# A fourth column tile in the opening rounds of an encoder layer's kernel, and y's second row tile loaded one slot sooner

## The chip, the cores and the metric

The kernel runs on one core of one Trainium2 chip. The metric is the time of one execution on the device in microseconds (us), the median of three runs. Five engines work beside each other, each in its own order, and wait for one another by semaphores: TensorE (PE; PEld is its weight load), VectorE (DVE), ScalarE (ACT), GpSimd (POOL) and SyncE (SP), which issues all DMAs here, one after the other.

## The reference

One layer of an encoder over 2048 tokens (a grid of 32 rows by 64 columns) of width 1024, in float32. In short:

```python
mod = silu(c) @ ada_w + ada_b                # shift, scale, gate
h = layernorm(x) * (1 + scale) + shift       # (2048, 1024)
proj = h @ w_in                              # (2048, 9216)
q_h, i_h, zf_fw, zf_bw, g_h, q_n, k_n, v_n, g_n = split(proj)
y_hg = hgrn2(q_h, i_h, zf_fw, zf_bw) * silu(g_h)       # 8 heads of 128, both directions
y_na = neighbourhood_attention(q_n, k_n, v_n, rpb) * silu(g_n)   # 16 heads of 64
y = concat(y_hg, y_na) @ w_out               # (2048, 2048) @ (2048, 1024)
x = layernorm(2**0.25 * x + gate * y) * ln_g + ln_b
```

## The kernel before

**Numbers.** A product in float32 is made of three matmuls: each operand is split into a high part (`hi`, a copy rounded to the format float32r, on ACT) and a low part (`lo`, the rest, a subtraction on DVE), and high x high, high x low and low x high are added up in PSUM. `proj_mm` (L274) does these three for one group k of 128 of the 1024 input columns and 512 tokens (128x512 each); eight such groups make one column tile of 128 projected columns. `vproj` (L280) does the same for the values, with 256 columns at a time.

**Stages.** The 2048 tokens are worked on in two halves of 1024, and each half in two groups g of 512. `startup` (L1181) makes h of the first half's groups 0 and 1 and projects the first attention pair (a pair is two attention heads; columns of keys, queries and gate, `NCOL0`) and its values. `first_half` (L1291) runs the attention of the first half for pairs 0 to 7 and, between its steps, projects the columns of the next pair (`first_stream`, L857). The linear recurrence of all heads follows, then the attention of the second half (phase `n1`, L1540) and the output part (phase `wo`, L1580): y, read back from DRAM, times w_out.

**The opening rounds.** The loop at L1261 goes over (g, k), 16 rounds. A round does, in the order of the code: its `jobs` (L1235: weight splits, sums of the modulation on DVE, statistics of x; in (0, 7) the rest of the statistics of group 1, its rates and the scaling of its rows); the four transposes of the next round's x (`turn_`, L232), its h on ACT (`high`, L237 and L239) and the low part on DVE (`low`, L1218); the nine matmuls of its own block, three column tiles i; in the last round of a group the evacuation of the three sums on ACT (`evac`, L772); and a step of `vproj`. In this stage the orders of PE, SP, ACT and DVE are those of the code (`manual_schedule`, L1387). So in (0, 7) PE comes to the transposes of round (1, 0), which need rows of group 1 that are scaled (L225), before it comes to the block of (0, 7).

**The stream of weights.** `Chunks` (L803) loads raw weight chunks of 128x512 through four buffers (`wraw`), splits them into four pairs of buffers (`whi`, `wlo`), and loads the next when one is split; `free` and `tick` say when.

**The weave.** In the later stages only PE's order is the code's; the other engines and SP's queue are ordered by a planner that works with estimates of times and with priorities. `weave` (L1359) lays pieces of a stream of projections between the steps of attention by a cost of 0.68 for each `proj_mm` (`KUS`) and a total; in `first_half` (L1338) the total of a stream is 48 such pieces (`NLEN`), and 10 of them go ahead of pair 0's first step. One attention tile is made of `scores` (L1023: matmuls, then minimum, powers and shares on DVE and ACT), `turned` (L1078: transposes, then copies of the turned probabilities on DVE, L1089, and ACT, L1091) and `sums` (L1095: matmuls with the values, L1107).

**Before the output part.** While pair 6 of the second half runs (u = 6, L1564), its `extra` jobs by slot load and split the first rows of w_out (`wo_load`, `wo_split`), and load the first row tiles of y (`y_early`, L1457, through the same four `wraw` buffers). A row tile is 128 tokens; the early part of a tile is two loads of 128x512 (q = 0, 1). `y_split` (L1462) makes the high parts on ACT (L1467) and the low parts on DVE (L1468). With u = 7, tile 1 is split and the stream between the attention steps is the first half of the output product for row tiles 0 to 3 (`out_stream`, L1486). Its weights on SP are the loads of L1430, the bias tables those of L730 to L738.

Of the kernel before, what the change touches and what calls it, by code (L numbers as in the profile page):

```python
# [11 lines left out]
F32R = mybir.dt.float32r  # L12
# [26 lines left out]
def body(ctx: ExitStack, tc: tile.TileContext, t):  # L39
# [240 lines left out]
    def vproj(src, dst, half, feed=None, fine=False):  # L280
        his, los = feed.take(4) if feed else load_split(lambda i: src[:, i * 512:(i + 1) * 512], 4)
        for t2 in range(2):
            pzs = [ps("pj"), ps("pj")]
            for k in range(KT):
                wh, wl = (w[k // 2][:, (k % 2) * 256:(k % 2 + 1) * 256] for w in (his, los))
                for tp in range(2):
                    for i in range(2):
                        g, o = divmod(((t2 * 2 + tp) * 2 + i) * P, GRP)
                        hh, hl = (hts[g, k, s][:, o:o + P] for s in range(2))
                        for n, (a, b) in enumerate(((hh, wh), (hh, wl), (hl, wh))):  # L290
                            pe.matmul(pzs[tp][:, i * 256:(i + 1) * 256], a, b, start=(k == 0 and n == 0 and i == 0), stop=(k == KT - 1 and n == 2), skip_group_check=True)  # L291
                if k % 2:
                    if k == KT - 1:
                        for tp, pz in enumerate(pzs):
                            v = tl("vo")
                            with tc.high_priority(offset=PRI):
                                (pinned if half else lambda x: x)(act.activation(v, pz, AF.Copy))
                                r0 = half * HALF + (t2 * 2 + tp) * 256
                                dma(dst[r0:r0 + 256].rearrange("(i p) c -> p i c", p=P), v.rearrange("p (i c) -> p i c", c=256))
                    if feed and t2:  # L300
                        feed.free(1)
                if fine or k % 2:
                    yield None
# [553 lines left out]
    def first_stream(st, feed):  # L857
# [6 lines left out]
        for n, c in NCOL0:  # L864
            his, los = feed.take(2)
            for g in range(2):
                pz = ps("pj")
                for k in range(KT):
                    proj_mm(pz, his, los, g, k)
                    if k == KT - 1:  # L870
                        st.raws[n][g] = evac(pz)
                        todo = [(n, g)]
                    if g == 1 and k % 4 == 3:
                        feed.free()
                    feed.tick()
                    if k == 1 and todo:
                        st.piece(*todo.pop())
                    yield KUS
# [302 lines left out]
    def startup():  # L1181
# [47 lines left out]
        for i in range(4):  # L1229
# [9 lines left out]
            (0, 3): [(mod_sum, 4), (w_split, 1, 1), (w_split, 2, 1)],  # L1239
            (0, 4): [(feed.split, 0), (mod_sum, 5)],  # L1240
            (0, 5): [(mod_sum, 6), (stat, 1, 0), (feed.split, 0)],
            (0, 6): [(mod_sum, 7), (stat, 1, 1)],
            (0, 7): [(stat, 1, 2), (stat, 1, 3), (rates, 1), (scale, 1, 0, 2)],
            (1, 2): [(scale, 1, 1, 4)],
        }
# [8 lines left out]
        values = vproj(t["w_v"][0], nv_d[0], 0, feed, True)  # L1254
        rows = {n: [None, None] for n, _ in NCOL0}
        order = [(g, k) for g in range(2) for k in range(KT)]
        turn_(0, 0)
        high(0, 0)
        w_split(0, 0)
        low(0, 0)  # L1260
        for n, (g, k) in enumerate(order):  # L1261
            for f, *a in jobs.get((g, k), []):
                f(*a)
            nxt = order[n + 1] if n + 1 < len(order) else None
            if nxt:
                turn_(*nxt)
            if nxt:
                high(*nxt)
                low(*nxt)
            if (g, k) == (0, 7):  # L1270
                feed.load(8)
                rp = bias_rows()
# [3 lines left out]
            if (g, k) == (1, 0):  # L1276
# [1 line left out]
                bias_tables(rp)  # L1278
                bias_pair(0)
                dma(c_d.rearrange("(p k) -> p k", k=KT), mod["c8"])  # L1280
            for i in (2, 0, 1) if g else (0, 1, 2):
                proj_mm(acc[i, g], *ws[i], g, k)
            if k == KT - 1:
                for i in range(3):
                    rows[NCOL0[i][0]][g] = evac(acc[i, g])
            next(values, None)
            if g:
                feed.tick()
        return rows, feed

    def first_half(raws, feed):  # L1291

        st = Prep(0, 0, raws)
        for n, g in (("k", 0), ("k", 1), ("q", 0), ("g", 0), ("q", 1), ("g", 1)):
# [39 lines left out]
        for w in range(8):  # L1334
            extra = {i: slots[4 * w + i] for i in range(4)}
            if w < 7:
                nxt = Prep(w + 1, 0, {n: [None, None] for n, _ in NCOL})
                dense, total, steps = first_stream(nxt, feed), NLEN + (0 if w % 2 == 0 else VLEN), 8  # L1338
            else:
                nxt, dense, total, steps = None, hgrn_dense(0, 0, feed=feed), HTOT, 10  # L1340
            r = weave(natten_woven(st, nxt, pipe, extra, w == 7), dense, total, steps, ahead=0 if w else AHEAD * KUS)[1]
# [43 lines left out]
    h_alloc()  # L1385
    with psum_phase("n0", NPS), tc.manual_schedule(engines={mybir.EngineType.PE}):
        with phase("st", SB_, SMS), tc.manual_schedule(engines={getattr(mybir.EngineType, e) for e in ("PE", "SP", "Activation", "DVE")}):  # L1387
            raws, feed = startup()
        with phase("n0", NB0, SM0):
            natten_init(4, 0)  # L1390
            st = first_half(raws, feed)

    def reload(g):
        for k in range(KT):
# [145 lines left out]
    with psum_phase("n1", NPS), phase("n1", NB1, SM1), tc.manual_schedule(engines={mybir.EngineType.PE}):  # L1540
# [15 lines left out]
        for u in range(8):  # L1556
            nxt, extra = None, None
            if u < 7:
# [4 lines left out]
                nxt = Prep(u + 1, 1, raws)  # L1563
                if u == 6:  # L1564
                    extra = {4: [(wo_load, 0, 0, 1)], 5: [(wo_load, 0, 2, 3, 4, 5)], 7: [(wo_split, 0, 0, 1)], 8: [(wo_split, 0, 2, 3), (wo_load, 0, 6, 7)],
                             9: [(y_early, 0), (wo_split, 0, 4, 5)], 10: [(y_split, 0), (wo_load, 1, 0, 1, 4, 5), (y_early, 1)]}
            else:
                y_split(1)
                dense, total = out_stream(list(range(NE))), NE * 16 * KUS
# [80 lines left out]
```

## Time and profile before

| | |
|---|---|
| median of 3 runs | 2619.01 us (2618.38 to 2622.39) |
| the profiled execution | 2618.81 us, span 2617.0 us |
| mean granted clock of TensorE | 0.993 |
| busy in the span | PE 2561.1 us, DVE 1736.9, ACT 1435.0, POOL 108.5 |
| DMA | 295.87 MB, mean 113 GB/s |

All times in the profile are from one execution, in us from the start of its span, those of single instructions also in ns. A timeline row has start, duration, engine, line, operation, what it writes and reads, its shape, the number of like instructions merged, and in brackets the idle time of the engine before it with what ended it. A row of waits has who waited for whom, total, number and longest. A row of windows has the stretch, its length, for each engine the busy time and the number of instructions, then the granted clock of TensorE as a share of full speed, the busy share of the DMA engines and the GB/s that they moved. A row of the chain has start, duration and what the path to the end went through. Matmuls are pipelined, and the durations shown overlap.

### The profile page before, as it was taken

How to read it: one execution, taken by the hardware profiler on the slowest of the kernel's cores; microseconds unless marked ns; L12 is line 12 of the kernel's file. 1: busy time of each engine (PE TensorE's matmuls, PEld its weight loads, DVE VectorE, ACT ScalarE, POOL GpSimd, SP SyncE). 2: the span in 40 equal slices, each digit the busy share in tenths (PEclk: the TensorE clock that was granted, in tenths of full speed). 3: DMA queues.
4: the chain of work that ended last, by engine and by line, in shares of the span. 5: the costliest groups of instructions: out<-in, count | busy, mean ns of one | idle time of the engine just before them, and what ended most of it. 6: DMA issues, size and time to landing. Idle time of an engine off the chain costs nothing.

```text
span 2617.0 us, 45804 instructions
## 1 busy us (share of the span) xinstructions
PE 2561.1 (98%) x17140; PEld 2146.7 (82%) x17140; DVE 1736.9 (66%) x4354; ACT 1435.0 (55%) x2857; POOL 108.5 (4%) x143
## 2 busy tenths in 40 slices
PE   6999999999999999999999999999999999899998
PEld 5888888878888888888888888898888887788887
DVE  7444545477777778877787788555777778558443
ACT  4533435376666566666766666455677777431110
POOL 0000000000000000000000000000000000042221
PEclk8999999999999999999999999999999999999999
DMA  7476455212211126212112222345455556443331
GB/s 273 141 211 143 128 169 152 97 55 72 65 65 58 65 69 213 90 49 81 62 60 71 74 80 73 113 125 153 129 137 144 137 139 171 126 153 129 97 97 57
DMA packets 225631, 295.87 MB, mean 113 GB/s; under 512 B 28807, under 2 KB 117511, under 8 KB 224263
## 3 DMA queue, kind: packets, MB, share of 16 engines
q1 hardware_dynamic: 225407, 292.93, 37.0%
q8 instruction: 135, 2.21, 0.4%
q14 instruction: 89, 0.73, 0.1%
HBM read 217.65 MB, written 66.99 MB: 109 GB/s over the span
## 4 chain that ended last, share of the span: by engine, by line
PE 90%; DVE 4%; DMA 3%; ACT 2%; issue 1%; SPq 0%; DVEq 0%; ACTq 0%
PE pj L278 51%; PE pj L291 5%; PE ps L1475 4%; PE ps L1477 4%; PE ps L1476 4%; PE ps L1107 3%; PE ps L1085 3%; PE ps L480 2%; PE ps L472 2%; PE ps L1036 1%; PE ps L547 1%; DMA bias<-tint 1%; PE ps L571 1%; PE ps L1043 1%; PE ps L573 1%; PE ps L519 1%
## 5 line engine op out<-in xcount | busy, mean ns | idle before, releaser
L278 PE MATMUL pj<-h,wh 128*128 128x512 f32 x4000 | 1274.4, 400 | 4.1 <-ACT wh L823 1.9
L278 PEld LDWEIGHTS pj<-h,wh 128*128 128x128 f32 x4000 | 725.7, 188 | 156.5 <-issue 13.8
L278 PE MATMUL pj<-h,wl 128*128 128x512 f32 x2000 | 784.6, 392 | 0.0
L278 PEld LDWEIGHTS pj<-h,wl 128*128 128x128 f32 x2000 | 376.0, 188 | 83.4 <-DVE wl L799 0.4
L1057 ACT ACTIVATE pbuf<-pbuf,mx 128x480 f32<-128x480 f32 (+5 forms) x256 | 152.4, 596 | 114.1 <-DVE mx L1052 113.2
L1052 DVE CUSTOM_DVE_ANT_1 pbuf<-ps,bias 128x480 f32<-128x480 f32 (+5 forms) x256 | 129.1, 540 | 101.0 <-PE ps L1041 43.2
L291 PE MATMUL pj<-wh,h 128*128 128x256 f32 x1024 | 195.7, 286 | 0.3 <-ACT e L772 0.3
L291 PEld LDWEIGHTS pj<-wh,h 128*128 128x128 f32 x1024 | 163.0, 191 | 4.0 <-issue 1.3
L269 DVE TENSOR_TENSOR wl<-wr,wh 128x512 fp32r<-128x512 f32 x192 | 131.3, 684 | 47.7 <-ACT wh L268 46.9
L268 ACT ACTIVATE wh<-wr 128x512 fp32r<-128x512 f32 x192 | 120.2, 626 | 73.7 <-PE pj L278 66.1
L291 PE MATMUL pj<-wl,h 128*128 128x256 f32 x512 | 144.7, 283 | 0.0
L1091 ACT ACTIVATE pt<-ps 120x384 f32<-120x384 f32 (+3 forms) x128 | 65.3, 510 | 119.1 <-PE ps L1085 118.7
L1089 DVE COPY pt<-ps 120x384 f32<-120x384 f32 (+3 forms) x128 | 74.9, 585 | 66.7 <-PE ps L1085 65.7
L1085 PE MATMUL ps<-ident,pbuf 128*128 128x128 f32 (+2 forms) x832 | 113.0, 273 | 4.5 <-DVE pbuf L1062 3.3
L1085 PEld LDWEIGHTS ps<-ident,pbuf 128*128 128x128 f32 (+2 forms) x832 | 96.5, 136 | 22.8 <-issue 2.3
L466 DVE TENSOR_TENSOR de<-e,de 128x512 f32<-128x512 f32 x64 | 44.2, 690 | 95.4 <-ACT de L465 95.4
L1451 ACT ACTIVATE yh<-yr 128x512 fp32r<-128x512 f32 x52 | 32.7, 628 | 132.9 <-PE ps L1476 115.7
L772 ACT ACTIVATE e<-pj 128x512 f32<-128x512 f32 x98 | 58.4, 596 | 82.9 <-PE pj L278 74.3
L1062 DVE TENSOR_SCALAR pbuf<-pbuf,mx 128x480 f32<-128x480 f32 (+5 forms) x256 | 101.0, 412 | 3.8
L1524 DVE TENSOR_TENSOR vt<-ps,gt 128x512 f32<-128x512 f32 x24 | 16.5, 692 | 130.5 <-PE ps L1477 130.5
L291 PEld LDWEIGHTS pj<-wl,h 128*128 128x128 f32 x512 | 97.9, 191 | 1.4 <-issue 0.5
L447 DVE TENSOR_TENSOR_SCAN c<-c,g 128x128 f32<-128x128 f32 x256 | 88.4, 404 | 10.7 <-ACT c L437 10.7
(277 smaller groups left out, 4684.4 us busy)
## 6 DMA issues: line engine op xcount, KB each, us to landing
wr<-in_w_in SPq DMA_DIRECT2D x276, 256.0 KB
yr<-yq SPq DMA_DIRECT2D x64, 256.0 KB
bias<-tint SPq DMA_DIRECT2D x24, 480.0 KB
x<-in_x SPq DMA_DIRECT2D x32, 256.0 KB
ada<-in_ada_m SPq DMA_DIRECT2D x8, 1024.0 KB
wr<-in_w_v SPq DMA_DIRECT2D x32, 256.0 KB
nv<-vt SPq DMA_DIRECT2D x32, 256.0 KB
hs<-s SPq DMA_DIRECT2D x32, 256.0 KB
```

Of the source, the lines that this page charges most:

```text
L268: act.activation(hi, raw, AF.Copy)
L269: dve.tensor_tensor(lo, raw, hi, op=ALU.subtract)
L278: pe.matmul(pz, a, b, start=(k == 0 and n == 0), stop=(k == KT - 1 and n == 2))
L291: pe.matmul(pzs[tp][:, i * 256:(i + 1) * 256], a, b, start=(k == 0 and n == 0 and i == 0), stop=(k == KT - 1 and n == 2), skip_group_check ...
L447: dve.tensor_tensor_scan(c[:, sl], c[:, sl], L[:, sl], 0.0, op0=ALU.add, op1=ALU.subtract)
L1052: return dve.tensor_tensor_reduce(s[:, 0:nk].rearrange("p (r c) -> p r c", c=kw), sc[:, 0:nk].rearrange("p (r c) -> p r c", c=kw), bt[:, 0 ...
L1057: act.activation(s[:, 0:nk], s[:, 0:nk], AF.Exp, scale=-1.0, bias=mx[:, 0:1], accum_out=mx[:, 1:2])
L1062: dve.tensor_scalar(s[:, 0:nk], s[:, 0:nk], mx[:, 2:3], 1.0, op0=ALU.mult, op1=ALU.mult)
L1085: pe.transpose(ptp[0:cw, c * P:(c + 1) * P], s[:, c * cw:(c + 1) * cw], ident)
L1475: pe.matmul(pz, yh[:, kk], wh, start=first, stop=False)
L1476: pe.matmul(pz, yh[:, kk], wl, start=False, stop=False)
L1477: pe.matmul(pz, yl[:, kk], wh, start=False, stop=last)
```

## The change

In `startup`, two more loads fetch the key columns of pair 1 (behind the last load of modulation weights). Their split into high parts is a new first job of round (0, 6) (`fourth_split`, ACT); the low parts follow in (0, 7) (`fourth_low`, DVE). Round (0, 7) has a new order: 14 matmuls of the fourth tile with high weights (k = 0 to 6); its own block, with each evacuation right behind its column tile; the jobs (statistics, rates, scaling of group 1); the small loads; the step of `vproj`; the two high matmuls of k = 7; the fourth tile's low parts on DVE; the transposes and h of round (1, 0); eight matmuls with low weights; the evacuation of the fourth tile; the evacuation of the values. To that end `vproj` yields once more before its last evacuation, and the loop drains it at its end. In group 1 too the evacuations stand right behind each column tile. The sum, `first`, is handed to `first_half`: `first_stream` of pair 1 leaves out the 24 matmuls of its first column tile and group 0, and the total for `weave` is 8 pieces less with w = 0.

In phase `n1`, `y_early` for row tile 1 moves from the end of slot 10 into slot 9, with row tile 0, and so ahead of four loads of w_out (`wo_load`, 1, 0, 1, 4, 5).

```diff
@@ -290,6 +290,8 @@
                         for n, (a, b) in enumerate(((hh, wh), (hh, wl), (hl, wh))):
                             pe.matmul(pzs[tp][:, i * 256:(i + 1) * 256], a, b, start=(k == 0 and n == 0 and i == 0), stop=(k == KT - 1 and n == 2), skip_group_check=True)
                 if k % 2:
+                    if fine and k == KT - 1:
+                        yield None
                     if k == KT - 1:
                         for tp, pz in enumerate(pzs):
                             v = tl("vo")
@@ -864,6 +866,9 @@
         for n, c in NCOL0:
             his, los = feed.take(2)
             for g in range(2):
+                if st.raws[n][g]:
+                    todo = [(n, g)]
+                    continue
                 pz = ps("pj")
                 for k in range(KT):
                     proj_mm(pz, his, los, g, k)
@@ -1239,7 +1244,7 @@
             (0, 3): [(mod_sum, 4), (w_split, 1, 1), (w_split, 2, 1)],
             (0, 4): [(feed.split, 0), (mod_sum, 5)],
             (0, 5): [(mod_sum, 6), (stat, 1, 0), (feed.split, 0)],
-            (0, 6): [(mod_sum, 7), (stat, 1, 1)],
+            (0, 6): [(lambda: fourth_split(),), (mod_sum, 7), (stat, 1, 1)],
             (0, 7): [(stat, 1, 2), (stat, 1, 3), (rates, 1), (scale, 1, 0, 2)],
             (1, 2): [(scale, 1, 1, 4)],
         }
@@ -1254,19 +1259,55 @@
         values = vproj(t["w_v"][0], nv_d[0], 0, feed, True)
         rows = {n: [None, None] for n, _ in NCOL0}
         order = [(g, k) for g in range(2) for k in range(KT)]
+        fourth, fraw = ([], []), [tl("raw"), tl("raw")]
+        for a in range(2):
+            dma(fraw[a], t["w_in"][NCOL0[0][1] // P + 1][:, a * 512:(a + 1) * 512])
+
+        def fourth_split():
+            w = tl("ada", F32R, [P, 2 * D])
+            for a in range(2):
+                hi, lo = (w[:, o:o + 512] for o in (a * 512, D + a * 512))
+                act.activation(hi, fraw[a], AF.Copy)
+                fourth[0].append(hi)
+                fourth[1].append(lo)
+
+        def fourth_low():
+            for a in range(2):
+                dve.tensor_tensor(fourth[1][a], fraw[a], fourth[0][a], op=ALU.subtract)
+
+        def fourth_mm(pz, k, low):
+            wh, wl = (w[k // 4][:, (k % 4) * P:(k % 4 + 1) * P] for w in fourth)
+            for n, (a, b) in enumerate(((wl, hts[0, k, 0]),) if low else ((wh, hts[0, k, 0]), (wh, hts[0, k, 1]))):
+                pe.matmul(pz, a, b, start=(k + n + low == 0), stop=(low == 1 and k == KT - 1))
+
+        def block(g, k):
+            for i in (2, 0, 1) if g else (0, 1, 2):
+                proj_mm(acc[i, g], *ws[i], g, k)
+                if k == KT - 1:
+                    rows[NCOL0[i][0]][g] = evac(acc[i, g])
+
         turn_(0, 0)
         high(0, 0)
         w_split(0, 0)
         low(0, 0)
         for n, (g, k) in enumerate(order):
+            if (g, k) == (0, 7):
+                pz = ps("po")
+                for kx in range(KT - 1):
+                    fourth_mm(pz, kx, 0)
+                block(g, k)
             for f, *a in jobs.get((g, k), []):
                 f(*a)
             nxt = order[n + 1] if n + 1 < len(order) else None
-            if nxt:
-                turn_(*nxt)
-            if nxt:
-                high(*nxt)
-                low(*nxt)
+
+            def ahead():
+                if nxt:
+                    turn_(*nxt)
+                    high(*nxt)
+                    low(*nxt)
+
+            if (g, k) != (0, 7):
+                ahead()
             if (g, k) == (0, 7):
                 feed.load(8)
                 rp = bias_rows()
@@ -1278,17 +1319,26 @@
                 bias_tables(rp)
                 bias_pair(0)
                 dma(c_d.rearrange("(p k) -> p k", k=KT), mod["c8"])
-            for i in (2, 0, 1) if g else (0, 1, 2):
-                proj_mm(acc[i, g], *ws[i], g, k)
-            if k == KT - 1:
-                for i in range(3):
-                    rows[NCOL0[i][0]][g] = evac(acc[i, g])
-            next(values, None)
+            if (g, k) != (0, 7):
+                block(g, k)
+            if (g, k) == (0, 7):
+                next(values)
+                fourth_mm(pz, k, 0)
+                fourth_low()
+                ahead()
+                for kx in range(KT):
+                    fourth_mm(pz, kx, 1)
+                first = evac(pz)
+                next(values)
+            else:
+                next(values, None)
             if g:
                 feed.tick()
-        return rows, feed
-
-    def first_half(raws, feed):
+        for _ in values:
+            pass
+        return rows, feed, first
+
+    def first_half(raws, feed, first):
 
         st = Prep(0, 0, raws)
         for n, g in (("k", 0), ("k", 1), ("q", 0), ("g", 0), ("q", 1), ("g", 1)):
@@ -1335,7 +1385,9 @@
             extra = {i: slots[4 * w + i] for i in range(4)}
             if w < 7:
                 nxt = Prep(w + 1, 0, {n: [None, None] for n, _ in NCOL})
-                dense, total, steps = first_stream(nxt, feed), NLEN + (0 if w % 2 == 0 else VLEN), 8
+                if w == 0:
+                    nxt.raws["k"][0] = first
+                dense, total, steps = first_stream(nxt, feed), NLEN + (0 if w % 2 == 0 else VLEN) - (0 if w else KT * KUS), 8
             else:
                 nxt, dense, total, steps = None, hgrn_dense(0, 0, feed=feed), HTOT, 10
             r = weave(natten_woven(st, nxt, pipe, extra, w == 7), dense, total, steps, ahead=0 if w else AHEAD * KUS)[1]
@@ -1385,10 +1437,10 @@
     h_alloc()
     with psum_phase("n0", NPS), tc.manual_schedule(engines={mybir.EngineType.PE}):
         with phase("st", SB_, SMS), tc.manual_schedule(engines={getattr(mybir.EngineType, e) for e in ("PE", "SP", "Activation", "DVE")}):
-            raws, feed = startup()
+            raws, feed, first = startup()
         with phase("n0", NB0, SM0):
             natten_init(4, 0)
-            st = first_half(raws, feed)
+            st = first_half(raws, feed, first)
 
     def reload(g):
         for k in range(KT):
@@ -1563,7 +1615,7 @@
                 nxt = Prep(u + 1, 1, raws)
                 if u == 6:
                     extra = {4: [(wo_load, 0, 0, 1)], 5: [(wo_load, 0, 2, 3, 4, 5)], 7: [(wo_split, 0, 0, 1)], 8: [(wo_split, 0, 2, 3), (wo_load, 0, 6, 7)],
-                             9: [(y_early, 0), (wo_split, 0, 4, 5)], 10: [(y_split, 0), (wo_load, 1, 0, 1, 4, 5), (y_early, 1)]}
+                             9: [(y_early, 0, 1), (wo_split, 0, 4, 5)], 10: [(y_split, 0), (wo_load, 1, 0, 1, 4, 5)]}
             else:
                 y_split(1)
                 dense, total = out_stream(list(range(NE))), NE * 16 * KUS
```

## What was predicted

> **What bounds the kernel now.** First the page: who is busy. Then the waits of PE alone, longest first, because only an idle PE can be filled.
>
> ```profile
> PE 2561.1 (98%) x17140; PEld 2146.7 (82%) x17140; DVE 1736.9 (66%) x4354; ACT 1435.0 (55%) x2857; POOL 108.5 (4%) x143
> ```
>
> ```profile
> PE ps L232 <- ACT x L225: 12.1, 6, 6.5
> PE ps L144 <- DVE ada L139: 5.7, 1, 5.7
> PE ps L1107 <- ACT pt L1091: 5.5, 1, 5.5
> ...
> PE pj L278 <- ACT wh L823: 1.9, 1, 1.9
> ```
>
> PE is busy 2561.1 of 2617.0 us; 55.9 us are left. The three longest single waits are 6.5, 5.7 and 5.5 us. The middle one is PE's first instruction, before anything has arrived. The others are the two places that the diff touches: the transposes of the second token group, and the sums of the last attention tile before the output part. No work is removed by the change, so it can gain only what these two waits cost. The profiled execution took 2618.81 us, 1.81 us around its span; the median of the runs is 2619.01 us, 0.20 us more, so I subtract from the median.
>
> **The first wait, with its aftermath.** The PE timeline at the start; columns are start, us, line, shape, count, and in brackets the idle time before:
>
> ```profile
> 34.63 0.60 PE L232 MATMUL ps<-ident,x 128*128 128x128 f32 x4
> ...
> 38.58 0.60 PE L232 MATMUL ps<-ident,x 128*128 128x128 f32 x4
> ...
> 51.74 0.28 PE L291 MATMUL pj<-wh,h 128*128 128x256 f32 x1
> 58.53 0.48 PE L232 MATMUL ps<-ident,x 128*128 128x128 f32 x1 [6.51 <-ACT x L225]
> ...
> 65.26 0.60 PE L232 MATMUL ps<-ident,x 128*128 128x128 f32 x4
> ```
>
> One round of the first stage (4 transposes, 9 projections, 12 value matmuls) takes 38.58 - 34.63 = 3.95 us. The round of step (0, 7) would begin at 51.86 (51.74 plus the 0.12 us at which these follow each other) and the next one begins at 65.26: 13.40 us, so 9.45 us are lost, 6.5 of them idle and the rest slow clock:
>
> ```profile
> 58.00:60.00 2.00, 1.24 (x5) 0.95 (x6) 0.54 (x2) 1.18 (x2) 0.00 (x0) 0.50 0.00 0
> ```
>
> The column behind the busy times is the granted clock: 0.50.
>
> **What the change puts there.** It moves 24 projection matmuls (pair 1, key columns, first 512 tokens) out of the first pair's stream into this round. Their price is a row of the chain for 24 of the same shape:
>
> ```profile
> 476.37 5.48 PE pj L278 x24
> ```
>
> 0.228 us each, 5.48 us in all, and the stream of the first pair is shorter by that. What the new round waits for is ACT's order, which the stage keeps as written; then, from the page, an evacuation (mean 596 ns):
>
> ```profile
> 50.96 0.78 ACT L237 ACTIVATE sg<-ps,shift,scale 128x512 f32<-128x512 f32 x1 [3.57 <-DVE scale L154]
> 51.78 0.63 ACT L239 ACTIVATE h<-sg 128x512 fp32r<-128x512 f32 x1
> 56.20 0.20 ACT L182 ACTIVATE l<-v 128x4 f32<-128x4 f32 x1 [3.79 <-DVE v L180]
> ...
> 57.66 1.52 ACT L225 ACTIVATE x<-x,xb,xr 128x512 f32<-128x512 f32 x2 [1.02 <-DVE xb L209]
> ```
>
> ```profile
> L772 ACT ACTIVATE e<-pj 128x512 f32<-128x512 f32 x98 | 58.4, 596 | 82.9 <-PE pj L278 74.3
> ```
>
> Step by step. PE begins with 14 high matmuls of the fourth tile: 51.86 + 14 x 0.228 = 55.05. Their two weight copies on ACT (0.63 us each, as the row of 51.78) fit into the 3.57 us idle before 50.96, provided that the two new loads have landed. They are issued behind the last modulation load, and the DMA stream is over by about 44:
>
> ```profile
> 44.00:46.00 2.00, 2.00 (x12) 1.70 (x12) 2.00 (x5) 0.05 (x1) 0.00 (x0) 1.00 0.10 39
> ```
>
> Only 39 GB/s are left there. Even at 300 GB/s 512 KB add 1.7 us: about 46, before ACT is free at 47.4 (50.96 - 3.57). Then the nine projections of block 7 (h ready at 52.4): 55.05 to 57.10. Here lies the **new wait**: the three evacuations of the block now stand on ACT ahead of the Ln of the rates (L182), which before ran at 56.20. The last of them starts about 0.25 us after the last matmul's end in cadence (a matmul's modelled end lies later than its successor's start), so 57.35, and ends 0.6 us later, at 57.95. From Ln to the scaled rows took 57.66 - 56.20 = 1.46 us, and PE started 58.53 - 57.66 = 0.87 us after that: 60.28. Behind the waiting Ln stand only the scale and the next h; PE meanwhile has 12 values and 2 high matmuls (to 59.0), so it idles about 1.3 us, and some 0.5 us more for ACT's second row. Four transposes end near 61.3, eight low matmuls near 63.15, and there the next round begins. The two extra subtractions on DVE fall behind its two scales and beside the transposes; the extra evacuation falls beside the next block. The next h (0.78 and 0.63 us on ACT behind 61.6) is ready at about 63.1 and its low half 0.7 us later, when PE needs them: nothing further is late.
>
> So the next round begins 65.26 - 63.15 = 2.1 us sooner although 5.48 us of matmuls lie in it: 7.6 us. Bounds: 9.4 us if the rates slip ahead of the evacuations and no idle time stays; 5.9 us if the remaining gap brings the slow clock again (1.7 us, half of the 3.4 us that the next rows show). On that the trace has a warning: the 1.9 us wait of L278, last row of the waits above, ends at 278.3, in a later pair, and behind it:
>
> ```profile
> 278.00:279.00 1.00, 0.71 (x2) 0.30 (x2) 0.73 (x2) 1.00 (x3) 0.00 (x0) 0.97 0.78 259
> ...
> 282.00:283.00 1.00, 1.00 (x5) 0.55 (x4) 0.00 (x0) 0.00 (x0) 0.00 (x0) 0.82 0.65 248
> ```
>
> The means 0.97 and 0.82 put half clock between 278.94 and 282.36, 3.4 us, after less than 2 us idle. My two gaps of 1.3 and 0.5 us are a little smaller and split by transposes, so I take no slow clock. The Trainium skill, "TensorE: Matmul & The Clock Gate", Part 1, says that the clock falls to half only after at least one idle window of about 3.4 us; by it no slow clock could follow here and the sum would be the same 7.6 us. The rows at 278 do not agree with that, and the measurement decides: the slow case keeps a chance.
>
> **The end of the first tokens' rounds.** Before, PE waited there for the value evacuation:
>
> ```profile
> 99.45 0.72 PE L278 MATMUL pj<-h,wh 128*128 128x512 f32 x2 [1.10 <-ACT vt L297]
> ```
>
> The change evacuates each block of the second group as it is done, not all three at the end, so ACT comes to the values sooner. Between 0 and 1.1 us; I take 0.4 us, nearer to 0 because ACT still copies keys there. The split of one weight chunk moves behind the loop; it is needed 12 matmul groups later, 8 us, and costs nothing. The first pair's stream has 8 fewer groups to lay between its attention steps: nothing, as long as the steps still cover each other (a rival below).
>
> **The second wait.** Before the output part, PE, ACT, SP:
>
> ```profile
> 2224.02 0.38 PE L1107 MATMUL ps<-pt,V 96*64 96x128 f32 x2
> 2229.92 0.47 PE L1107 MATMUL ps<-pt,V 96*64 96x128 f32 x1 [5.51 <-ACT pt L1091]
> ```
>
> ```profile
> 2226.10 0.63 ACT L1467 ACTIVATE yh<-yr 128x512 fp32r<-128x512 f32 x1 [4.82 <-DMA yr<-yq]
> 2227.82 0.63 ACT L1467 ACTIVATE yh<-yr 128x512 fp32r<-128x512 f32 x1 [1.10 <-DMA yr<-yq]
> ...
> 2229.40 0.47 ACT L1091 ACTIVATE pt<-ps 96x384 f32<-96x384 f32 x1
> ```
>
> ```profile
> 2198.25 0.52 SPq L1441 DMA_DIRECT2D yr<-yq  x1
> ...
> 2215.83 1.25 SPq L1441 DMA_DIRECT2D yr<-yq  x2
> ```
>
> PE waits for a copy of turned probabilities, which ACT has queued behind the split of y's row tile 1, which waits for loads issued at 2215.83. Row tile 0 went out at 2198.25. With both in one slot, tile 1 follows at once, as soon as its two buffers are free (the last weight split, around 2200). It moves past four w_out loads and a bias table on SP and past nothing that PE waits for. Even with the same 12 us of flight (2215.83 to 2227.8) it lands by 2212, nine before ACT is ready for it. ACT, free at 2221.3 (2226.10 - 4.82), then runs without 4.82 + 1.10 us of waiting, and the copy ends at about 2223.9, just before PE asks for it at 2224.1. The idle goes, and the slow clock after it:
>
> ```profile
> 2200.11 1.68 PE ps L1107 x28
> ...
> 2235.28 0.66 PE ps L1085 x6
> ```
>
> Between 2224.14 and 2235.28 PE does 10 sums (0.06 us each, from 28 in 1.68) and 12 projections at 0.228: 3.35 us of work in 11.14 us, 7.8 us lost. I take 7.4: the copy comes within half a microsecond of the need. What is late next is DVE, whose split of y moves forward by the same amount. From there to the end each load hangs on buffers that PE frees, so the shift stays. Bounds: 0 (below) to 7.8.
>
> **Sum.** 7.6 + 0.4 + 7.4 = 15.4 us: 2619.0 - 15.4 = 2603.6 us, -0.6%.
>
> **Rivals.** (a) *Tile 1 of y is no sooner*: SP puts its loads where they were, behind the w_out loads, or another item of ACT's queue ends as late. For it: SP's order in this stage is a planner's, by its own estimates. Against: the emission moves ahead of those loads, and the two items of ACT between y's split and the copy, a gate and a w_out split, run back to back in the trace. Then only the start gains: 2619.0 - 8.0 = 2611.0 us.
>
> (b) *The start gains less*: the remaining gap trips the clock (1.7 us), or the engines that the planner orders fall otherwise in the shorter first pair and repeat a gap as at 278 (1.9 us and 1.7 us of half clock). 2605.3 to 2609 us.
>
> (c) *Slower, by thinner cover*: in the first pair, PE has (48 - 10) x 0.68 / 8 = 3.23 us of projections between two attention half-steps by the planner's costs; the change leaves (40 - 10) x 0.68 / 8 = 2.55. If scores, powers and shares need more than that, PE idles at each of 8 half-steps. From about 1.9 us each (15.4 / 8) this alone eats the gain, and gaps of that size halve the clock, as at 278; some 34 us of the first pair would then take up to 17 more: up to 2621 us with no idle counted, and about 2626 us with 5 us of it. Against: behind the first pair not one such wait shows,
>
> ```profile
> 120.00:180.00 60.00, 60.00 (x404) 52.77 (x403) 25.27 (x76) 22.46 (x52) 1.01 (x4) 1.00 0.66 194
> ```
>
> 60.00 us busy of 60.00, DVE and ACT under half, and each chain has three half-steps to run in.
>
> (d) *The moved matmuls only fill*: the start's wait shifts behind the fourth tile with its full length, because the rates come later by as much. Then the 5.48 us are not gained, only y: 2611.6 us. Against: the rates slip by 57.95 - 56.20 = 1.75 us only.
>
> **Chances.** Forecast (2600.5 to 2605) 0.62; (b) 0.14; (a) or (d) 0.11; more than forecast 0.04; within 0.2% (5.2 us, about what a measurement of this kernel can tell from no change) 0.05; (c) 0.04. The range 2600 to 2611.7 holds the first three. Faster by over 0.2%: 0.91; same 0.05; slower 0.04.
>
> **What would show it.** In the changed trace: 14 projections in place of the 6.51 us, then a gap of 1 to 2 us before the transposes, granted clock 1.00 throughout; the first attention scores some 7 us sooner; the L1467 copies without a wait for a load, no 5.5 us gap at L1107, and no 0.50 clock behind it. Wrong it would be if the loads of the fourth tile land after ACT asks for them, if the clock falls at the rest of the gap, if the first pair's attention shows waits of PE, or if y's second tile is still issued behind the w_out loads.

## The result, and the profile after

The changed kernel takes 2614.70 us (median of 22 runs, 2609.84 to 2616.25) and the kernel before, run beside it, 2618.64 us (22 runs, 2613.23 to 2622.39). The ratio is 0.9984, with a 95% interval of 0.9977 to 0.9990: 4.2 us faster (2.6 to 6.0). The forecast was 15.4 us. The profiled execution took 2612.69 us, with a span of 2610.9 us.

Lines have moved in the changed kernel: the turned copies stand at L1096 and the sums at L1112, the projections of the output at L1527 to L1529, `wo_split` at L1487 (ACT) and L1488 (DVE), `y_split` at L1519, the loads of w_out at L1482 and of y at L1493, the store of y at L1123.

First the page's line of busy engines and the waits of PE, longest first (who waited for whom: total, times, longest).

```profile
PE 2561.6 (98%) x17140; PEld 2146.3 (82%) x17140; DVE 1737.8 (67%) x4356; ACT 1435.4 (55%) x2859; POOL 108.4 (4%) x143
```

```profile
PE ps L232 <- ACT x L225: 7.5, 6, 5.6
PE ps L144 <- DVE ada L139: 5.7, 1, 5.7
PE pj L1527 <- ACT wo L1487: 3.3, 1, 3.3
...
PE ps L278 <- ACT h L239: 1.6, 2, 1.1
```

Of the two waits that the change aimed at, the 5.5 us of the sums are gone from the list, and the 6.5 us of L232 too (the 5.6 us left are the first transposes of all, at 15.00). Two rows are new or longer: 3.3 us for a high copy of w_out, and 1.1 us for an h. They are the story of this case.

**The opening**, PE's timeline of round (0, 7) and the granted clock over it:

```profile
52.68 3.36 PE L1281 MATMUL ps<-h,ada 128*128 128x512 f32 x14
...
59.36 0.63 PE L1281 MATMUL ps<-h,ada 128*128 128x512 f32 x2
...
60.95 0.33 PE L232 MATMUL ps<-ident,x 128*128 128x128 f32 x1 [0.96 <-ACT x L225]
61.65 0.55 PE L232 MATMUL ps<-ident,x 128*128 128x128 f32 x3 [0.38 <-ACT x L225]
61.96 2.09 PE L1281 MATMUL ps<-h,ada 128*128 128x512 f32 x8
63.88 0.60 PE L232 MATMUL ps<-ident,x 128*128 128x128 f32 x4
```

```profile
52.00:64.00 12.00, 10.66 (x59) 8.73 (x58) 7.92 (x21) 6.19 (x11) 3.44 (x5) 1.00 0.35 121
```

Fourteen projections stand where PE was idle, the gap is down to 0.96 and 0.38 us, the clock column says 1.00, and the round takes 63.88 - 52.68 = 11.20 us where it took 13.40, with the 5.48 us of moved matmuls in it.

**Thirty us later**, PE and ACT at the last round of the second group:

```profile
94.02 0.50 PE L278 MATMUL ps<-h,vt 128*128 128x512 f32 x1 [1.11 <-ACT h L239]
94.88 0.50 PE L278 MATMUL ps<-h,vt 128*128 128x512 f32 x1 [0.36 <-DVE h L1223]
...
99.04 0.73 PE L278 MATMUL pj<-h,wh 128*128 128x512 f32 x2 [0.62 <-ACT vt L299]
```

```profile
92.05 0.61 ACT L978 ACTIVATE KA<-e 64x512 fp32r<-64x512 f32 x1
92.69 0.63 ACT L978 ACTIVATE KB<-e 64x512 fp32r<-64x512 f32 x1
93.34 0.63 ACT L239 ACTIVATE h<-sg 128x512 fp32r<-128x512 f32 x1
```

Two copies of attention keys stand on ACT ahead of the last h, for which PE waits. They are the keys of pair 1: the fourth tile made their sums ready at 64, so the planner could draw the copies forward. In before they ran at 105.87, and PE's wait at that place was 0.23 us:

```profile
94.80 0.50 PE L278 MATMUL ps<-h,vt 128*128 128x512 f32 x1 [0.23 <-DVE h L1218]
```

```profile
105.87 0.63 ACT L973 ACTIVATE KA<-e 64x512 fp32r<-64x512 f32 x1
```

**The output part**: ACT, the store and the loads on SP, PE.

```profile
2215.63 1.14 ACT L1519 ACTIVATE yh<-yr 128x512 fp32r<-128x512 f32 x2
2217.95 0.63 ACT L1487 ACTIVATE wo<-vt 128x512 fp32r<-128x512 f32 x1 [0.66 <-DMA vt<-in_w_out]
2218.48 0.47 ACT L1096 ACTIVATE pt<-ps 96x384 f32<-96x384 f32 x1
...
2241.27 0.63 ACT L1487 ACTIVATE wo<-vt 128x512 fp32r<-128x512 f32 x1 [4.13 <-DMA vt<-in_w_out]
```

```profile
2232.11 0.42 SPq L1482 DMA_DIRECT2D vt<-in_w_out  x1
...
2234.15 0.32 SPq L1123 DMA_DIRECT2D yq<-vt  x1
...
2238.31 0.33 SPq L1482 DMA_DIRECT2D vt<-in_w_out  x1
```

```profile
2241.95 0.79 PE L1527 MATMUL pj<-wo,yh 128*128 128x512 f32 x1 [3.29 <-ACT wo L1487]
```

The next transposes of PE, in before and in the changed kernel:

```profile
2235.12 0.82 PE L1085 MATMUL ps<-ident,pbuf 128*120 128x128 f32 x6
```

```profile
2221.98 0.82 PE L1090 MATMUL ps<-ident,pbuf 128*120 128x128 f32 x6
```

The split of y runs without a wait, the turned copy ends at 2218.95 as PE needs it, and PE comes to these transposes 13.14 us sooner. Twenty us later it stands for 3.29 us and then runs at half clock (0.79 us for this matmul; 0.50 behind a wait at full clock, in a run below), because ACT waits 4.13 us for w_out's last weight tile: that load was issued at 2238.31, behind the end of a store of y. When the half clock is over PE is 6.45 us ahead, where it was 5.54 ahead at 2213. Of the 7.6 us that the move brought (13.14 less 5.54), 0.9 are left.

### The profile page after: what moved, and what is told of

Same layout as the page of the kernel before. It is cut to its first block, busy times and chain, and to the rows that moved or that the text cites. A ratio compares the mean times of both kernels' runs of the same rounds, so it can differ in the third digit from the quotient of the medians.

```text
span 2610.9 us, 45808 instructions
## 1 busy us (share of the span) xinstructions
PE 2561.6 (98%) x17140; PEld 2146.3 (82%) x17140; DVE 1737.8 (67%) x4356; ACT 1435.4 (55%) x2859; POOL 108.4 (4%) x143
## 4 chain that ended last, share of the span: by engine, by line
PE 90%; DVE 4%; DMA 3%; ACT 2%; issue 1%; SPq 0%; DVEq 0%; ACTq 0%
PE pj L278 51%; PE pj L291 5%; PE ps L1527 4%; PE ps L1528 4%; PE ps L1529 4%; PE ps L1112 3%; PE ps L1090 3%; PE ps L482 2%; PE ps L1041 2%; PE ps L474 2%; PE ps L549 1%; PE ps L573 1%; PE ps L1048 1%; PE ps L575 1%; PE ps L521 1%; PE ps L653 1%
## 5 line engine op out<-in xcount | busy, mean ns | idle before, releaser
L1096 ACT ACTIVATE pt<-ps 120x384 f32<-120x384 f32 (+3 forms) x128 | 65.2, 509 | 121.0 <-PE ps L1090 120.7
```

## The experiments

All kernels compute the whole output. Each was timed against before on its own chip, where before takes 2616.2 to 2616.8 us; "us" is the ratio less 1, times 2616.5.

| kernel | median us | ratio (95%) | us |
|---|---|---|---|
| full change, again | 2613.19 | 0.9988 (0.9979 to 0.9997) | -3.1 |
| opening alone | 2610.61 | 0.9970 (0.9958 to 0.9982) | -7.8 |
| y move alone | 2619.96 | 1.0011 (1.0003 to 1.0020) | +2.9 |
| order of round (0, 7) alone | 2613.03 | 0.9988 (0.9979 to 0.9997) | -3.1 |
| full, k = 6, 7 of w_out in tag gt | 2608.84 | 0.9967 (0.9955 to 0.9979) | -8.6 |
| full, k = 7 alone in tag gt | 2608.64 | 0.9972 (0.9961 to 0.9984) | -7.3 |
| opening, and tag gt | 2611.11 | 0.9975 (0.9966 to 0.9984) | -6.5 |
| y move, and tag gt | 2616.07 | 0.9998 (0.9989 to 1.0007) | -0.5 |
| full, key copies in order | 2611.74 | 0.9981 (0.9973 to 0.9990) | -5.0 |
| full, tag gt, copies in order | 2607.94 | 0.9966 (0.9954 to 0.9978) | -8.9 |
| opening, copies in order | 2608.36 | 0.9966 (0.9952 to 0.9979) | -8.9 |
| full, k = 7 in gt, copies in order | 2606.71 | 0.9961 (0.9948 to 0.9973) | -10.2 |

Some executions differ by 5 us and more from the median of their kernel, so the traces are compared over two stretches that leave the rest out. The *opening stretch* runs from PE's first transpose of x to the first turned copy on ACT, the *output stretch* from the evacuation below to the statistics of the first finished row tile (rows of the full change; the same instructions in each kernel).

```profile
116.69 0.49 ACT L1096 ACTIVATE pt<-ps 96x384 f32<-96x384 f32 x1 [0.56 <-PE ps L1090]
...
2199.21 0.60 ACT L774 ACTIVATE e<-pj 128x512 f32<-128x512 f32 x1
...
2332.27 1.27 DVE L1578 BATCH_NORM_STATS2 bnst<-xt 128x6 f32<-128x512 f32 x2
```

Opening stretch: 105.0 to 105.9 us in the three kernels with the old opening, 102.6 with the order alone, 101.7 in all six with the new opening, 100.2 to 100.3 in all four that also keep the key copies in order. With the new opening the stretch holds 235 of the 128x512 matmuls, without the fourth tile 223; so 12 matmuls, 2.7 us at 0.228, have to be taken off the 101.7 to compare it with the others. Output stretch: 131.1 to 134.5 (mean 132.8, five kernels) with y late; 133.1 to 135.5 (mean 134.4, four) with y early; 128.8 to 131.6 (mean 130.2, five) with y early and tag gt.

**Which part gained?** The opening alone (slot 10 as before) and the y move alone (the opening as before).

```diff
-  9: [(y_early, 0, 1), ...], 10: [(y_split, 0), (wo_load, 1, 0, 1, 4, 5)]
+  9: [(y_early, 0), ...], 10: [(y_split, 0), (wo_load, 1, 0, 1, 4, 5), (y_early, 1)]
```

> The opening rounds' change alone; y's tile 1 loads stand in slot 10 as before. Theory A (the opening works and keeps what it gains; the output part gives its gain back): in the trace of the changed kernel PE stands 5.4 us ahead of before from the second token group on, and 5.5 us ahead at the transposes at 2213.46, so this kernel is about 5.5 us faster than before (2613 us), all of what the full change brings, and the 5.5 us wait of the sums before the output part is back. Rival B (the start's gain is lost on the way, the full change's 3.9 us come from y): between 0 and 2 us faster. Rival C (most of the start's lead is swallowed by a later start: the first transposes stood at 15.00 instead of 14.20 because of this change): the first transposes stand near 15.0 again; if they stand near 14.2 the 0.8 us were this one execution's.

> The y loads' move alone; the opening rounds as before. Theory A (gain given back at the w_out loads): the 5.51 us wait at the sums is gone, PE reaches the transposes behind it about 7.8 us sooner, and then waits 3 to 4 us for a high copy of w_out whose load stands on SP behind a store of y, with half clock behind it: about 1 us faster in all (0 to 2). Rival B (the move brings all of the full change's gain): 4 to 7 us faster, with no such wait.

The opening alone is 7.8 us faster (4.7 to 11.0), the y move alone 2.9 us slower (0.8 to 5.2); the sum, 4.9, agrees with the 4.2 (2.6 to 6.0) of the full change. Theory A had the opening right and the sign of the y move wrong: it had expected 1 us of gain. The wait it foretold is there (3.32 us at 2251.41). The opening alone has its wait back, and its SP queue tells why the y move can't gain; PE first, then SP:

```profile
2222.99 0.32 PE L1112 MATMUL ps<-pt,V 96*64 96x128 f32 x1 [3.68 <-ACT pt L1096]
```

```profile
2232.28 0.45 SPq L1482 DMA_DIRECT2D vt<-in_w_out  x1
...
2234.36 0.33 SPq L1123 DMA_DIRECT2D yq<-vt  x1
...
2238.66 0.33 SPq L1482 DMA_DIRECT2D vt<-in_w_out  x1
```

PE is 5.5 us later here than with y early, and yet the same three transfers go out within 0.4 us of the times above. SP's queue doesn't follow PE; it waits for transfers of its own. The waits of SP in the full change from 2210 to 2245:

```profile
SPq L979 <- DMA bias<-tint: 5.0, 1, 5.0
...
SPq L1482 <- DMA yq<-vt: 3.3, 1, 3.3
SPq L989 <- DMA bias<-tint: 2.6, 1, 2.6
```

The chain existed before, with the same wait for the store (first row); ACT then found its weights there (second row, without a bracket), because PE was late:

```profile
SPq L1430 <- DMA yq<-vt: 4.2, 2, 3.4
```

```profile
2248.63 1.14 ACT L1435 ACTIVATE wo<-vt 128x512 fp32r<-128x512 f32 x2
```

The first transposes stood at 15.29 and 15.07 us in these two, at 14.20 in before's profile, at 14.16 to 15.29 over all: rival C isn't needed, since the kernel with the old opening has it too. It is the landing of the fourth of x's eight first loads (the second half of the second row tile; not of the third tile, as an expectation below has it). DVE's statistics wait for it 0.28 to 1.42 us in twelve traces, and not in the two with the earliest transposes. In the opening alone:

```profile
8.91 0.69 DVE L202 BATCH_NORM_STATS2 bnst<-x 128x6 f32<-128x512 f32 x1 [1.35 <-DMA x<-in_x]
```

**Is it the loads of w_out?** The last two weight tiles take the two buffers of tag gt, which are free earlier.

```diff
-  tl("wr2" if k in (4, 5) else "wr")
+  tl("wr2" if k in (4, 5) or (n and k > 5) else "wr")
-  1: [(wo_split, 1, 0, 1), (wo_load, 1, 6, 7)], 2: [(wo_split, 1, 2, 3, 4, 5)]
+  1: [(wo_split, 1, 0, 1, 4, 5), (wo_load, 1, 6, 7)], 2: [(wo_split, 1, 2, 3)]
```

> The full change, and the last two weight tiles of w_out's second half (k = 6, 7) loaded into the two buffers of tag gt, whose splits (k = 4, 5) come one slot sooner; the loads then wait neither for a split at 2231.25 nor for the store of y. Theory A (the wait at 2241.95 took the gain of the y move): that wait of 3.29 us and the half clock behind it go; 4 to 6.5 us faster than the full change, 8 to 11 us faster than before. Rival D (the wait passes on once more: to the split of y's next tile at 2266.31, or to the stores and loads of the last stage): the 3.29 us go, another wait of PE of 2 us or more appears behind it, and the time stays within 2 us of the full change.

The wait of PE is gone; ACT's split of both tiles waits less than a microsecond:

```profile
2238.98 1.27 ACT L1487 ACTIVATE wo<-gt 128x512 fp32r<-128x512 f32 x2 [0.94 <-DMA gt<-in_w_out]
```

8.6 us faster than before, 4.4 more than the full change, as A said; the output stretch falls to 128.84.

**Which link?** Only k = 7 leaves the buffer that the store of y holds.

```diff
-  tl("wr2" if k in (4, 5) else "wr")
+  tl("wr2" if k in (4, 5) or (n and k > 6) else "wr")
-  1: [(wo_split, 1, 0, 1), (wo_load, 1, 6, 7)], 2: [(wo_split, 1, 2, 3, 4, 5)]
+  1: [(wo_split, 1, 0, 1, 4), (wo_load, 1, 6, 7)], 2: [(wo_split, 1, 2, 3, 5)]
```

> The full change, and only the last weight tile of w_out's second half (k = 7) through a buffer of tag gt, freed by the split of k = 4 one slot sooner; k = 6 still waits on SP for the split that frees its vt buffer at about 2231. That takes away one link alone: the load that stood behind the store of y. Theory A (the store of y is the link that makes the 3.3 us wait): both loads go out within a microsecond of each other near 2232, the wait for w_out's high copy falls from 3.3 us to 0 to 1.3 us, and the kernel gains most of what the run with both tiles in tag gt gained: 3 to 5 us faster than the full change, 6.5 to 9 us faster than before. Rival J (the split that frees k = 6's buffer is the late link, and the store only followed): the wait stays at 2 us or more and the time within 1.5 us of the full change.

SP and PE:

```profile
2234.20 0.42 SPq L1482 DMA_DIRECT2D vt<-in_w_out  x1
2234.73 0.37 SPq L1482 DMA_DIRECT2D gt<-in_w_out  x1
```

```profile
2239.43 0.50 PE L1527 MATMUL pj<-wo,yh 128*128 128x512 f32 x1 [1.13 <-ACT wo L1487]
```

Both loads go out together, at 2234 and not near 2232 as A had it, and the wait falls to 1.13 us, with no half clock in the whole output stretch; 7.3 us faster than before. So J is out, and the store of y is the link that makes the last load late.

**Is the y move worth anything, then?** Two kernels cross the parts: the free loads with y late, and the free loads and y early without the new opening (their diffs are those above).

> The opening's change and w_out's tiles through tag gt, but y's tile 1 loaded in slot 10 as before. Theory A (the y move is worth something only where the w_out loads are free; and the free loads are worth nothing while the sums wait for y): the wait of the sums of 3.7 to 5.5 us is there again, no wait for w_out, and the time is that of the opening alone (about 6 to 8 us faster than before), 2 to 4 us slower than both with the y move. Rival G (the y move hurts by itself, whatever the w_out loads do): this kernel is as fast as the full change with tag gt, or faster.

> The opening as before; y's tile 1 one slot sooner, and w_out's last two tiles through tag gt. Theory A (the y move is worth something once its successors in the queue are free): the stretch from the end of slot 10 to the last stage, 131 to 134.5 us with y late and 133 to 135.5 with y early, falls to about 129 to 130.5 as in the two runs with tag gt; 2 to 5 us faster than before, where the y move alone was 2.9 us slower. Rival F (the free loads helped only beside the changed opening, by the place of the clock's windows): within 1.5 us of before.

With y late the sums wait 5.05 us again (first row) and no wait for w_out follows; the time, 6.5 us faster, is that of the opening alone. Its interval overlaps that of the kernel with both, so it is the output stretch that speaks (134.5 against 128.8, from one trace each; the means of the two groups are 132.8 and 130.2). With y early and the old opening (second and third row) two small waits stay:

```profile
2226.36 0.48 PE L1112 MATMUL ps<-pt,V 96*64 96x128 f32 x1 [5.05 <-ACT pt L1096]
```

```profile
2227.59 0.32 PE L1107 MATMUL ps<-pt,V 96*64 96x128 f32 x1 [1.18 <-ACT pt L1091]
...
2247.99 0.49 PE L1475 MATMUL pj<-wo,yh 128*128 128x512 f32 x1 [1.80 <-ACT wo L1435]
```

That one gained 0.5 us only (2.9 faster to 1.8 slower), where A expected 2 to 5: by the time, this is what rival F named. It is 3.4 us better than the y move alone, and its stretch is 131.6, the longest of its group, against 134.7. So the free loads mend what the y move cost; that the two together are worth something beside the old opening isn't shown.

**What does the order of round (0, 7) do by itself?** No fourth tile; block and evacuations ahead of the jobs (the loads and functions of the fourth tile, also gone, are left out here).

```diff
 if (g, k) == (0, 7):
-    pz = ps("po")
-    for kx in range(KT - 1):
-        fourth_mm(pz, kx, 0)
     block(g, k)
...
     next(values)
-    fourth_mm(pz, k, 0)
-    fourth_low()
     ahead()
-    for kx in range(KT):
-        fourth_mm(pz, kx, 1)
-    first = evac(pz)
     next(values)
```

> Only the new order of round (0, 7) and the evacuations behind each column tile; no fourth tile (its 24 matmuls stay in pair 1's stream), y as before. Theory A (the order takes a part of the wait by itself, since the block no longer stands behind the transposes; the fourth tile's matmuls fill the rest): block and values fill 3.4 us, PE then waits 2 to 3 us for the scaled rows, and some half clock may follow; 3 to 5 us faster than before, 2 to 4 us slower than the opening's change in full. Rival H (all comes from the moved matmuls): same time as before within 1 us. Rival I (the matmuls only fill, all comes from the order): as fast as the opening's change in full.

PE's waits in it:

```profile
59.08 0.33 PE L232 MATMUL ps<-ident,x 128*128 128x128 f32 x1 [1.80 <-ACT x L225]
59.79 0.98 PE L232 MATMUL ps<-ident,x 128*128 128x128 f32 x7 [0.38 <-ACT x L225]
61.87 1.52 PE L278 MATMUL ps<-h,vt 128*128 128x512 f32 x2 [1.09 <-ACT h L239]
```

Theory A: 3.1 us faster (0.8 to 5.5), under half of the opening's gain. With two more waits of 0.41 and 0.22 us ahead of the block, PE idles 3.90 us in this round, against 6.74 before (6.51 and 0.23) and 1.34 in the full change (0.96 and 0.38), and half clock follows (two matmuls in 1.52 us). So the order takes somewhat under half of the idle time, and the fourth tile's matmuls fill most of the rest and keep the clock full.

**Are the key copies the wait at 94?** Pair 1's first key copies are kept in the program's order.

```diff
-  keep = pinned if src in self.bk or self.first else lambda x: x
+  keep = pinned if src in self.bk or self.first or (self.half == 0 and self.p == 1 and i == 0) else lambda x: x
```

> The full change, with one difference: the copies of pair 1's first keys (which the fourth tile makes ready 40 us sooner) are kept in the program's order on ACT, so that they can't be drawn ahead of the last h of the opening rounds. Theory A (these copies made the new waits of 1.11 and 0.36 us at 94.02 and 94.88): both waits fall to the 0.23 us of before and the first pair starts about 1.2 us sooner; 1 us faster than the full change. Rival E (ACT is late there for another reason, as the order of the evacuations): the waits stay, same time as the full change within 0.5 us.

ACT and PE:

```profile
91.98 0.62 ACT L239 ACTIVATE h<-sg 128x512 fp32r<-128x512 f32 x1
```

```profile
93.38 0.50 PE L278 MATMUL ps<-h,vt 128*128 128x512 f32 x1 [0.22 <-DVE h L1223]
```

The h is made 1.36 us sooner and both waits are down to one of 0.22. The opening stretch is 1.5 us shorter in each of the four kernels with this line. The time shows it less surely: 0.8 us better than the full change, inside the interval.

**Together, and once more.**

> The two mends together: the full change, w_out's last two tiles through the buffers of tag gt, and pair 1's first key copies kept in program order. Theory A (the two give-backs are separate waits of PE and add up): 4.2 us in the output part (from the trace of the run with tag gt) and 1.5 us at the opening's end (from the trace of the run with the kept order), so 5 to 6 us faster than the full change and 9 to 11 us faster than before. Rival F (they fall into the same slack or a clock spell takes their place): no faster than the run with tag gt alone, that is about 7.5 us faster than before.

> The opening's change with pair 1's first key copies in program order; y's tile 1 in slot 10 as before. Theory A (the whole gain of the change is the opening's; without the give-back at the last h it is 1.5 us more, and the y move isn't missed): 8 to 10 us faster than before, about 1.5 us faster than the opening's change alone; the wait of the sums of 3 to 5.5 us is there. Rival G (the y move is needed for a gain of that size): at most 7 us faster.

> The full change, w_out's k = 7 through tag gt, and the kept order of pair 1's first key copies: the version that the runs so far point to. Theory A: the two add up, 9 to 10.5 us faster than before (the run with k = 7 alone was 7.3 us faster, and the kept order brings 1.5 us). Rival F (one eats the other): no faster than the run with k = 7 alone, about 7 us.

> The changed kernel unaltered, on the chip of the other runs of this call: 3 to 6 us faster than before. Theory A: its trace shows the waits for w_out's high copy (3.3 us, with half clock behind it) and the 1.1 us wait for the last h again, and the first transposes at about 15.0, since the load of x's third tile comes late in most executions. Rival C: the first transposes near 14.2 as in before's profile.

The first is 8.9 us faster (A said 9 to 11, F 7.5: not settled by the time). The second says that the y move isn't missed: 8.9 us without it, as A expected, and its wait of 4.38 us at 2224.42 is there. The third is the fastest seen, 10.2 us (7.1 to 13.6), as A said; its interval overlaps those of the other two. The unaltered change gave 3.1 us again, with the waits of 3.26 us (w_out) and 1.1 us (h), and its first transpose at 14.72. Its sums still waited 1.24 us at 2217.90; in four of the nine traces with y early they wait 1.18 to 1.77 us, in the others 0.6 or less.

## Why the prediction was wrong

**What bounded the kernel** was read rightly: the two waits were there to be taken, and both were taken in the profiled execution. The measured gain of 4.2 us is the case "within 0.2%", to which the prediction gave 0.05 and no mechanism.

**The opening, 7.6 us:** right. The round became 2.20 us shorter (forecast 2.1) with 5.48 us more work in it. The gaps were 0.96 and 0.38 us (forecast 1.3 and 0.5), the clock stayed full; their sum, 1.34, is below the 1.77 us of idle that the last section finds ahead of 45 of 47 falls of the clock. The forecast sum, 1.8, would have been at that edge, and to that extent the choice of full clock was lucky. Rival (d) fell: the rates slipped, but the waits shrank.

**The end of the first rounds, 0.4 us:** the wait for the value evacuation went from 1.10 to 0.62, 0.5 us. The prediction closed that stage with "nothing further is late". That failed: 1.11 + 0.36 us stand ahead of it, less the 0.23 us of before, 1.24 us lost. It had asked what the moved matmuls free on PE, and not what their finished sum lets the planner start on ACT. Altogether 2.20 + 5.48 + 0.48 - 1.24 = 6.9 us, and 7.8 (4.7 to 11.0) by the time of the opening alone; that this is so near to the forecast 8.0 is in part luck.

**The wait before the output part, 7.4 us:** this is the step that failed. The wait went and PE was 7.6 us further ahead behind it, as worked out (the prediction took 2235.28, a row of the chain, as the start of before's transposes; PE's timeline has 2235.12, so its 7.8 is 7.6). The step that carries it to the end was: "What is late next is DVE, whose split of y moves forward by the same amount. From there to the end each load hangs on buffers that PE frees, so the shift stays." The last load of w_out hangs on a buffer that a store of y frees, and SP reaches that store by a queue of its own waits, at 2234 whether PE is early or late. In place of the 5.51 us wait PE then has one of 3.29 us, with half clock behind it. In place of 7.4 us gained, the move cost 2.9 us alone, 3.6 beside the opening (7.8 less 4.2) and 3.9 beside the opening with the key copies in order (8.9 less 5.0). The lower bound of that term, 0, stood for loads that are no sooner (rival a), and nothing stood for a wait that is handed on.

The output stretch shows why nothing was gained. With y late the sums wait 3.1 to 5.5 us (mean 4.35, five traces); with y early the matmuls of the output wait 3.25 to 3.32 us for w_out (four traces). PE's whole idle time in the stretch is 7.0 to 9.4 us (mean 8.2) with y late and 7.4 to 8.9 (mean 7.8) with y early, and both waits have 3.4 or 6.8 us of half clock at them. Why the move even costs 2.9 us isn't settled. With y early the half clock is longer, 6.8 to 10.2 us (mean 8.5) against 3.4 to 6.8 (mean 5.5), and the stretch is 1.6 us longer in the mean, with ranges that overlap. But most of that comes from a spell of 3.4 us behind a wait of 1.74 us that every kernel has before the transposes of slot 10: three of the four traces with y early have this spell, none of the five with y late. No run tells whether that is the move's doing or only where the wait lay on the grid that the last section describes.

**The rivals.** (a) didn't happen: y's second tile went out at 2196.90. The times of (a) and (d), 2611.0 and 2611.6, came nearest all the same, since both gave up one of the two terms; but none of the rivals had the wait handed on to the next load. Before's own waits of SP held the row for it, 3.4 us for the store of y, 25 us behind the place where the prediction stopped looking at that queue. (c) didn't show: PE was busy 60.00 of 60.00 us from 120 to 180.

## What to carry to other kernels

A wait that is removed hands its engine on to whatever was landing in its shadow: before a shift is carried to the end, list the transfers that land within that shift of their use, and follow each back through its queue until it hangs on the engine that was freed; one that doesn't caps the gain. Work that is done sooner also makes its successors ready sooner, and a planner that orders by readiness may put them in front of something that the critical engine needs; hold them back by name. And test the parts of a change apart: here one part carried the gain, 7.8 us, and the other took back 2.9 to 3.9.

## What the runs showed of the hardware

The granted clock falls to half on a fixed grid. In all 14 traces (from 30 us on, without the last 20 us) its spells are 3.413 us long or a multiple, and within one trace they begin at whole multiples of 3.413 us from each other. Each trace was cut by its grid, and PE's idle time summed in each window. Of 47 windows followed by a fall, 45 had 1.77 us of idle or more; of the windows at full clock not followed by one, all but three had 1.73 us or less (the three: 1.87 to 1.94). So about half a window of idle is enough, and the same gap costs or not by where it lies. The wait of 1.90 us for a weight split, in before and in the full change with the key copies in order, each with the windows behind it:

```profile
278.29 0.73 PE L278 MATMUL pj<-h,wh 128*128 128x512 f32 x2 [1.90 <-ACT wh L823]
```

```profile
278.96:282.36 3.40, 3.40 (x9) 2.67 (x9) 1.21 (x3) 0.33 (x1) 0.00 (x0) 0.50 0.74 226
```

```profile
270.93 0.73 PE L278 MATMUL pj<-h,wh 128*128 128x512 f32 x2 [1.90 <-ACT wh L825]
```

```profile
270.90:274.30 3.40, 3.37 (x14) 2.26 (x15) 1.95 (x4) 1.02 (x2) 0.00 (x0) 1.00 0.69 207
```

Clock 0.50 behind the one, 1.00 behind the other. Ten of the 14 traces have the fall there, four don't. The full change itself had the fall there in one trace (at 274.64) and not in the other. So a part of the difference between executions of one kernel can come from this: 3.413 us at half clock are 1.7 us of work lost for each such window.

The Trainium skill, "TensorE: Matmul & The Clock Gate", Part 1, gives windows of 3413 ns that run freely and don't reset when a kernel starts: the length of the spells here agrees. It also gives the fall as following an idle window; here windows only half idle were enough (1.77 us of 3.413).

Also unexpected: how far the first transposes of x move from execution to execution, from 14.16 to 15.29 us, with the landing of the fourth load of x.
